# FFN's last projection: five of the eleven row pairs as seven block products instead of eight

## The chip, the cores and the metric

The kernel runs on one core of one Trainium2 chip. The metric is the device time of one execution in microseconds (us), as the median of several runs. A core has a matrix engine (TensorE, PE in the profile, with its weight loads as PEld), three engines for element-wise work (VectorE or DVE, ScalarE or ACT, GpSimd or POOL) and a queue that issues transfers (SyncE or SP). Each engine works through its own instructions in order and waits for the others by semaphores. SBUF is the working memory, PSUM the banks that PE writes its sums to.

## The reference

The reference is one block of a streaming encoder on 512 tokens with 1024 features: attention and a gated recurrence in parallel, merged, and then a feed-forward network with a final norm. Only its end matters here:

```
D_FF = ((8 * D_MODEL // 3 + 255) // 256) * 256          # 2816
...
        hn = rmsnorm(h, norm_ffn_g[l])
        gu = hn @ w_ffn_in[l]
        g, up = jnp.split(gu, 2, axis=-1)
        h = h + (jax.nn.silu(g) * up) @ w_ffn_out[l]
    return rmsnorm(h, final_norm_g)
```

So the last projection multiplies 512 x 2816 activations with a 2816 x 1024 matrix, adds the result to `h`, and each row of `h` is normed.

## The kernel before

Every float32 operand is split into a high part and a low remainder (`split`, L78): ACT writes the high part, DVE (or POOL, in `split_act`) subtracts it from the source to get the low one. A product of two such operands is three matmuls into the same PSUM sums (`mm3`, L72): high by high, high by low, low by high.

The 2816 rows of the last weight matrix are 22 tiles of 128, or eleven pairs. `act2[i]` holds the activations of pair i, transposed: 128 rows, two tiles, 512 tokens. The output is four tiles of 128 tokens (t) by two halves of 512 columns (cc). For the first half of the columns the loop (L1073 to L1098) goes over chunks of four row tiles; for each it takes the split weights (`weights`, L1084), and `out_tile` (L1038) adds its share to the four PSUM banks `po_out0` to `3` (tag `mm`, four banks). Activations are the stationary operand, 512 weight columns the moving one. Then `h_out` (L1044) adds each bank to `h`, squares it for the norm and multiplies by the norm's gain. The second half does the same with the last token tile cut into two pieces of 256 columns; its last chunks run piece by piece, so that each token tile can be normed and written out while the next one is still in PE.

Weights come in the order of `plan` (L94). `prefetch` takes them ahead of use: SP loads a piece of 512 KB into one of three `raw` buffers (`load`, L137), ACT and DVE split it into a `whl` buffer (four in the pool `wp`, more in another pool for some pieces, `extra`). A load waits until DVE has read the buffer's previous content, a split until PE has used the previous content of its `whl` buffer. `barrier` limits how far ahead this goes.

Before this stage the gate and up projections run as block products (`block_product`, L258): two by two blocks, seven products for eight. The last of them (`fu20`) ends among the first matmuls of the output stage. A framework orders the instructions of every engine by priorities and its own estimate of time; only the attention's PE order is fixed by hand (`manual_schedule`, L858). `split_act` (L1003) splits the activations; for pairs 0, 1, 2 and 4 POOL makes the low part.

Of the kernel before, what the change touches and what calls it, by code (L numbers as in the profile page):

```python
# [8 lines left out]
F32 = mybir.dt.float32  # L9
F32R = mybir.dt.float32r  # L10
# [4 lines left out]
P = 128  # L15
D = 1024
S = 512
KT = D // P
NT = S // P
# [3 lines left out]
FT = DFF // P  # L23
# [7 lines left out]
V_CW, V_CB, V_BR, V_BI, V_LAM, V_BM, V_GF = 0, 32, 40, 48, 56, 64, 80  # L31
NV = 88
CW = 256


@with_exitstack
def block_kernel(ctx: ExitStack, tc: tile.TileContext, x, norm_mix_g, w_in, b_merge, rel_table,
# [34 lines left out]
    def mm3(o, sh, sl, mh, ml, start, stop, parts=False):  # L72

        pe.matmul(o, sh, mh, start=start, stop=False, skip_group_check=parts)  # L74
        pe.matmul(o, sh, ml, start=False, stop=False, skip_group_check=parts)  # L75
        pe.matmul(o, sl, mh, start=False, stop=stop, skip_group_check=parts)  # L76

    def split(hi, lo, src):  # L78

        act.activation(hi, src, AF.Copy)  # L80
        dve.tensor_sub(lo, src, f(hi))  # L81
# [4 lines left out]

    def cols(src, col, width=CW):
        return (src, col, width)

    chunks = []  # L90
# [37 lines left out]
    for cc in range(2):  # L128
        for k0 in range(0, FT, 4):
            plan(f"fo{cc}_{k0}", cols(w_ffn_out, cc * S, S), rows=k0 * P, kts=min(4, FT - k0))  # L130

    made = []
    whole, every = slice(0, CW), slice(0, S)
# [27 lines left out]
    def weight_sums(name, ahead=False):  # L161
# [55 lines left out]
                blocks_[key] = o[:, i]  # L217
        return blocks_

    def prefetch(n):  # L220
        while len(made) < min(n, len(chunks), index.get(barrier[0], len(chunks))):
            name, parts, rows, kts = chunks[len(made)]
            if name in strassen:
                made.append(weight_sums(name))
                continue
            tiles = []
            wide = sum(width for *_, width in parts)
            step = 4 * CW // wide
            for k in range(0, kts, step):
                n_ = min(step, kts - k)  # L230
                if name in extra:
                    hl = extra[name].tile([P, 2, n_, wide], F32R, tag="whl", bufs=4, name=f"whl_{name}_{k}")
                else:
# [31 lines left out]

    def block_product(name, i, right, c):

        w = weights(name)
        p = ps.tile([P, 256], F32, tag="mm", bufs=4, name=f"p_{name}")
        q = ps.tile([P, 2, 256], F32, tag="st"[i % 2], bufs=2, name=f"q_{name}")  # L270
        a, b = (tg_.tile([P, 2, 256], F32, tag="tg", name=f"keep{n}_{name}") for n in "ab")

        def keep(o, src):
            act.activation(o, src, AF.Copy)
# [12 lines left out]
        dve.tensor_add(c[:, 0:2], q[:], a[:])  # L287
        product(p[:], w["a22"], right["t4"], False)
        keep(c[:, 2], p[:])
# [712 lines left out]

    def split_act(i):  # L1003
        o = act2[i]
        pl, bufs = (acp, 13) if i == 0 else (ohp, 6) if i < 7 else (op, 4)
        hi = pl.tile([P, 2, S], F32R, tag="act", bufs=bufs, name=f"act_hi{i}")
        lo = acp.tile([P, 2, S], F32R, tag="act", bufs=13, name=f"act_lo{i}")
        act.activation(hi[:], o[:], AF.Copy)  # L1008
        (pool if i in (0, 1, 2, 4) else dve).tensor_sub(lo[:], o[:], f(hi[:]))  # L1009
        for c in range(2):  # L1010
            actT[2 * i + c] = (hi[:, c], lo[:, c])
# [13 lines left out]
    hn_stack.close()  # L1025


    ohp = ctx.enter_context(pool_of("act_hi", 6, "right"))
    op = ctx.enter_context(pool_of("out", 4, "right"))
    for i, name in enumerate(n for n, *_rest in chunks if n.startswith("fo")):  # L1030
        if i % 4 >= 2:
            extra[name] = op
# [5 lines left out]
    def out_tile(t, po, k0, wf, at):  # L1038
        for k in range(min(4, FT - k0)):
            kk = k0 + k  # L1040
            mm3(po[:, 0:at.stop - at.start], actT[kk][0][:, t * P:(t + 1) * P], actT[kk][1][:, t * P:(t + 1) * P],
                wf(0, k, at), wf(1, k, at), kk == 0, kk == FT - 1)

    def h_out(cc, t, po, eng, i, at):  # L1044

        n = slice(cc * S + at.start, cc * S + at.stop)
        hs = ht[t][:, n]
        dve.tensor_add(hs, po[:, 0:at.stop - at.start], hs)
        junk = op.tile([P, S], F32, tag="junk", bufs=2, name=f"oj{t}_{i}")
        act.activation(junk[:, 0:at.stop - at.start], hs, AF.Square, accum_out=osq[t][:, i:i + 1])  # L1050
        eng.tensor_mul(hs, hs, g_fin[:, n])

    def out_norm(t, parts):

        part = cp.tile([P, 1], F32, tag="part", bufs=2, name=f"part{t}")
        if parts > 1:
            dve.tensor_reduce(part[:], osq[t][:, 0:parts], mybir.AxisListType.X, ALU.add)
            dve.tensor_scalar(part[:], part[:], 1.0 / D, EPS, ALU.mult, ALU.add)
        else:
            dve.tensor_scalar(part[:], osq[t][:, 0:1], 1.0 / D, EPS, ALU.mult, ALU.add)  # L1060
        return part

    def h_norm(t, part, i):
        sd = cp.tile([P, 1], F32, tag="sd", bufs=4, name=f"osd{t}")
        act.activation(sd[:], osq[t][:, i:i + 1], AF.Sqrt, bias=part[:], scale=1.0 / D)
        rs = cp.tile([P, 1], F32, tag="rs", bufs=4, name=f"ors{t}")
        dve.reciprocal(rs[:], sd[:])
        act.activation(ht[t][:, 0:384], ht[t][:, 0:384], AF.Copy, scale=rs[:, 0:1])
        dve.tensor_scalar(ht[t][:, 384:], ht[t][:, 384:], rs[:, 0:1], None, ALU.mult)
# [3 lines left out]
    ks = list(range(0, FT, 4))  # L1073
    late = 4
    for cc, tags in enumerate(("mmmm", "sstmm")):

        pieces = [(t, every) for t in range(NT)] if cc == 0 else [*((t, every) for t in range(3)), (3, slice(0, CW)), (3, slice(CW, S))]
        pos = [ps.tile([P, S], F32, tag={"m": "mm"}.get(tag, tag), bufs=4 if tag == "m" else 2, name=f"po_out{cc}_{i}")
               for i, tag in enumerate(tags)]
        for k0 in ks[:late] if cc else ks:  # L1080
            if cc == 0:
                for i in range(max(1, k0 // 2), min(k0 + 4, FT) // 2):
                    split_act(i)
            wf = weights(f"fo{cc}_{k0}", 3)  # L1084
            for (t, at), po in zip(pieces, pos):
                out_tile(t, po, k0, wf, at)
        if cc == 0:
            for (t, at), po in zip(pieces, pos):
                h_out(0, t, po, pool, 0, at)
    wfs = [weights(f"fo1_{k0}", 0) for k0 in ks[late:]]  # L1090
    for i, ((t, at), po) in enumerate(zip(pieces, pos)):
        for k0, wf in zip(ks[late:], wfs):
            out_tile(t, po, k0, wf, at)
        n = 1 + i // 4
        if i != 3:
            part = out_norm(t, n)
        h_out(1, t, po, dve, n, at)
        if i != 3:  # L1098
            h_norm(t, part, n)


# [23 lines left out]
```

## Time and profile before

| what | us |
|---|---|
| median of three runs (880.00 to 880.09) | 880.01 |
| the profiled execution's own time | 879.88 |
| its span, first to last instruction | 878.0 |
| PE busy | 868.9 |
| DVE busy | 545.3 |
| ACT busy | 471.4 |
| POOL busy | 115.1 |
| first output matmul starts | 746.75 |
| last output matmul starts | 871.6 |

The span is what the profile shows of one execution; the time also holds what lies around it, 1.88 us in this one. Times in the rows are counted from the span's start. A row of the timeline has the start, the duration, the engine, the line, the operation, and what is written from what; a number behind x says how many instructions were merged into it, and brackets tell how long the engine stood idle before and what ended that. Matmuls overlap: each is shown for longer than the distance to the next one, so the rate is read from starts. A row of the windows has, for each engine, busy time and (x) instructions, and at its end the clock granted to PE, the DMA engines' share and GB/s.

### The profile page before, as it was taken

Reading aid. Unit: us, or ns where it says so; the run is one execution under the profiler, and the core shown is the slowest. Engines: PE = TensorE matmul, PEld = TensorE weight load, DVE = VectorE, ACT = ScalarE, POOL = GpSimd, SP = SyncE. Lnnn points to the kernel's source line nnn. Section 1 sums busy time; section 2 is a strip of 40 time slices with the busy share of each in tenths; the row PEclk is TensorE's granted clock in tenths of the full one; section 3 lists DMA queues with packets and bytes.
Section 4 is the critical chain, followed back from the end, with each engine's and each line's share of the span. In section 5 each row is a group of like instructions: output and inputs, shape, how many; then the busy total and the mean of one; then the engine's idle time right before and its main releaser. Section 6 shows DMA issues by size and latency. Waiting matters only on the chain.

```text
span 878.0 us, 13349 instructions
## 1 busy us (share of the span) xinstructions
PE 868.9 (99%) x5220; PEld 775.8 (88%) x5220; DVE 545.3 (62%) x843; ACT 471.4 (54%) x827; POOL 115.1 (13%) x172
## 2 busy tenths in 40 slices
PE   9999999999999999999999999999999999999997
PEld 7988888888889889898888889999999999888886
DVE  5676456553456675766566557888888786554203
ACT  7586556642256675767633357555555555723103
POOL 3512212120113132322100000000000001401100
PEclk9999999999999999999999999999999999999999
DMA  8133322323332232332224622333333432363002
GB/s 285 56 121 98 94 81 88 121 96 96 108 97 84 85 96 73 97 97 61 74 95 131 229 94 74 110 109 97 97 96 112 127 100 72 113 198 120 26 1 97
DMA packets 86143, 90.10 MB, mean 103 GB/s; under 512 B 5456, under 2 KB 74672, under 8 KB 86080
## 3 DMA queue, kind: packets, MB, share of 16 engines
q1 hardware_dynamic: 84480, 85.73, 31.1%
q10 hardware_dynamic: 1376, 3.47, 1.1%
q8 instruction: 41, 0.67, 0.3%
q14 instruction: 22, 0.18, 0.1%
q0 software_dynamic: 224, 0.05, 0.0%
HBM read 87.10 MB, written 2.14 MB: 102 GB/s over the span
## 4 chain that ended last, share of the span: by engine, by line
PE 95%; DVE 2%; POOL 1%; ACT 1%; issue 0%; DMA 0%; ACTq 0%; DVEq 0%; POOLq 0%
PE po_out L74 4%; PE po_out L76 4%; PE po_out L75 4%; PE p_fg L76 2%; PE p_fg L75 2%; PE p_fg L74 2%; PE p_fu L75 2%; PE p_fu L76 2%; PE p_fu L74 2%; PE pT L806 2%; PE o L826 2%; PE po_v L74 2%; PE po_v L76 2%; PE po_v L75 2%; PE po_xr L75 2%; PE po_xr L74 2%
## 5 line engine op out<-in xcount | busy, mean ns | idle before, releaser
L75 PE MATMUL po_out<-whl_fo,act_hi 128*128 128x512 f32 (+1 forms) x198 | 72.4, 366 | 0.0
L74 PE MATMUL po_out<-whl_fo,act_hi 128*128 128x512 f32 (+1 forms) x198 | 72.4, 366 | 0.0
L76 PE MATMUL po_out<-whl_fo,act_lo 128*128 128x512 f32 (+1 forms) x198 | 71.7, 365 | 0.0
L81 DVE TENSOR_TENSOR whl_fo<-raw_fo,whl_fo 128x1024 fp32r<-128x1024 f32 x22 | 28.8, 1317 | 45.7 <-ACT whl_fo L80 45.2
L795 POOL TENSOR_SCALAR p<-p,rl 128x128 f32<-128x128 f32 (+1 forms) x64 | 36.9, 596 | 134.8 <-DVE rl L793 134.5
L1009 POOL TENSOR_TENSOR act_lo<-act,act_hi 128x1024 fp32r<-128x1024 f32 x4 | 11.4, 2842 | 324.0 <-ACT act_hi L1008 322.6
L80 ACT ACTIVATE whl_fo<-raw_fo 128x1024 fp32r<-128x1024 f32 x22 | 23.1, 1058 | 47.0 <-PE po_out L76 33.5
L75 PEld LDWEIGHTS po_out<-whl_fo,act_hi 128*128 128x128 f32 x198 | 37.4, 189 | 6.0
L76 PEld LDWEIGHTS po_out<-whl_fo,act_lo 128*128 128x128 f32 x198 | 37.3, 189 | 6.0
L74 PEld LDWEIGHTS po_out<-whl_fo,act_hi 128*128 128x128 f32 x198 | 37.4, 189 | 5.9
L792 ACT ACTIVATE p<-p,m 128x128 f32<-128x128 f32 (+1 forms) x64 | 35.8, 561 | 12.1 <-DVE m L791 11.8
L74 PE MATMUL po_v<-whl_v,xnT 128*128 128x256 f32 x128 | 36.5, 285 | 0.0
L76 PE MATMUL po_v<-whl_v,xnT 128*128 128x256 f32 x128 | 36.2, 283 | 0.0
L75 PE MATMUL po_v<-whl_v,xnT 128*128 128x256 f32 x128 | 36.2, 283 | 0.0
L791 DVE CUSTOM_DVE_ANT_0 p<-s,bias 128x128 f32<-128x128 f32 (+1 forms) x64 | 29.1, 484 | 1.0 <-PE s L783 1.0
L81 DVE TENSOR_TENSOR whl_qk<-raw_qk,whl_qk 128x1024 fp32r<-128x1024 f32 x16 | 20.9, 1307 | 13.4 <-ACT whl_qk L80 13.4
L81 DVE TENSOR_TENSOR whl_fu_s<-s_fu,whl_fu_s 128x1024 fp32r<-128x1024 f32 x20 | 24.1, 1222 | 6.2 <-ACT whl_fu_s L80 6.2
L81 DVE TENSOR_TENSOR pp<-pT,pp 128x384 fp32r<-128x384 f32 (+1 forms) x48 | 27.6, 597 | 0.5 <-ACT pp L80 0.4
L75 PE MATMUL po_xr<-xnT,whl_xr 128*128 128x512 f32 (+1 forms) x80 | 27.7, 353 | 0.0
L75 PE MATMUL po_gr<-xnT,whl_gr 128*128 128x512 f32 (+1 forms) x80 | 27.5, 347 | 0.0
L76 PE MATMUL po_gr<-xnT,whl_gr 128*128 128x512 f32 (+1 forms) x80 | 27.3, 347 | 0.0
L76 PE MATMUL po_xr<-xnT,whl_xr 128*128 128x512 f32 (+1 forms) x80 | 27.2, 346 | 0.0
(428 smaller groups left out, 3055.0 us busy)
## 6 DMA issues: line engine op xcount, KB each, us to landing
raw_fg<-in_w_ffn_in_dram SPq DMA_DIRECT2D x24, 512.0 KB, 4.2
raw_fu<-in_w_ffn_in_dram SPq DMA_DIRECT2D x22, 512.0 KB, 3.9
raw_fo<-in_w_ffn_out_dram SPq DMA_DIRECT2D x22, 512.0 KB, 4.4
raw_qk<-in_w_in_dram SPq DMA_DIRECT2D x32, 256.0 KB, 3.1
raw_xr<-in_w_in_dram SPq DMA_DIRECT2D x8, 512.0 KB, 3.7
raw_gr<-in_w_in_dram SPq DMA_DIRECT2D x8, 512.0 KB, 3.5
raw_ga<-in_w_in_dram SPq DMA_DIRECT2D x8, 512.0 KB, 3.6
raw_gb<-in_w_in_dram SPq DMA_DIRECT2D x8, 512.0 KB, 3.5
```

The source lines that it names most:

```text
L74: pe.matmul(o, sh, mh, start=start, stop=False, skip_group_check=parts)
L75: pe.matmul(o, sh, ml, start=False, stop=False, skip_group_check=parts)
L76: pe.matmul(o, sl, mh, start=False, stop=stop, skip_group_check=parts)
L80: act.activation(hi, src, AF.Copy)
L81: dve.tensor_sub(lo, src, f(hi))
L791: dve.tensor_tensor_reduce(prob[qb][:], scs[qb][:, 0:w], bias[:, S - w:S], -1.0, 3e38, ALU.add, ALU.min, nmax[:, qb:qb + 1])
L792: act.activation(prob[qb][:], prob[qb][:], AF.Exp, bias=nmax[:, qb:qb + 1], scale=-1.0, accum_out=lsum[:, qb:qb + 1])
L795: pool.tensor_scalar(prob[qb][:], prob[qb][:], rl[:, qb:qb + 1], 1.0, ALU.mult, ALU.mult)
L806: pe.transpose(pt[:, at * P:(at + 1) * P], prob[qb][:, kb * P:(kb + 1) * P], ident[:])
L826: pe.matmul(po[:, S - n:S], st, pp[i][:, part, lo:lo + n], start=kb == 0 and part == 0, stop=kb == NT - 1 and part == 1)
L1009: (pool if i in (0, 1, 2, 4) else dve).tensor_sub(lo[:], o[:], f(hi[:]))
```

## The change

Pairs 0 to 5 stay as they were (`plain`). Pairs 6 to 10 (`paired`) become block products in the form of Strassen and Winograd: the two 256-token halves and the two row tiles of a pair make a two by two matrix of activation blocks, the two row tiles and the two column halves one of weight blocks; seven products of blocks (256 tokens by 128 rows by 512 columns) give the four blocks of the output. Each product is six matmuls of 512 columns, where the pair had 48 in all.

- Weights: for a `paired` pair the pieces are `fo0` (both tiles of the first column half, as before), `t12` (T1 = w12 - w11 and T2 = w22 - T1), `t3b` (w22 - w12, and w22) and `t4` (w21 - T2), all made by `out_sums` with DVE subtractions, from three loads of 512 KB (one of them that of `fo0`) and two of 256 KB (`half`). Seven `whl` buffers are shared in a ring of seven (`out_home`): four in `wp`, three in the pool `out`.
- Activations: `a_first` splits the first token half of a pair into `left`; `a_sums` makes the sums of the activation blocks on DVE and splits them into `right`; `a_second` overwrites `left` and `a_last` part of `right` with the remaining differences. `spread` deals these out between the pairs' matmuls.
- Order: PE's order in the stage is fixed by hand: `fo0` of the plain pairs, `fo0` of the paired ones, three plain `fo1`, `t12`, three plain `fo1`, `t3b`, `t4`. Sums that several outputs share stay in PSUM (`p_out`, `q_out`) and are added to `h` at several points by `h_add`. The second column half is normed first; the last piece is the first column half of token tile 3, cut into two pieces of 256 columns.
- Chunks are one pair each now, `barrier` stops at `fo0_3`, and the last block product (`fu20`) reads two pieces ahead instead of one.

```
+N_PLAIN = 6
+OUT_TILES = (N_PLAIN - 1) + 2 * (11 - N_PLAIN)
...
+    for i in range(FT // 2):
+        plan_out(0, i)
+    for i in plain[:N_PLAIN // 2]:
+        plan_out(1, i)
+    for i in paired:
+        plan_block("t12", i)
+    for i in plain[N_PLAIN // 2:]:
+        plan_out(1, i)
+    for i in paired:
+        plan_block("t3b", i)
+    for i in paired:
+        plan_block("t4", i)
...
+    def out_home(name):
+        n = out_count[0] = out_count[0] + 1
+        pl, bufs = (wp, 4) if n % 7 in (1, 2, 3, 4) else (out_room[0], 3)
+        return pl.tile([P, 2, 2, S], F32R, tag="whl", bufs=bufs, name=f"whl_{name}")
...
+        if kind == "t12":
+            raw = wp.tile([P, 2, S], F32, tag="raw", bufs=3, name=f"raw_{name}")
+            sp.dma_start(out=raw[:], in_=w_ffn_out[rows:rows + P, :].rearrange("p (c n) -> p c n", c=2))
+            b22 = half_row(S)
+            t2 = t2_of[i] = out_room[0].tile([P, S], F32, name=f"t2_{i}")
+            t1 = raw[:, 1]
+            dve.tensor_sub(t1, raw[:, 1], raw[:, 0])
+            dve.tensor_sub(t2[:], b22, t1)
+            split(hl[:, 0, 0], hl[:, 1, 0], t2[:])
+            split(hl[:, 0, 1], hl[:, 1, 1], t1)
+        elif kind == "t3b":
+            raw = wp.tile([P, 2, S], F32, tag="raw", bufs=3, name=f"raw_{name}")
+            sp.dma_start(out=raw[:], in_=w_ffn_out[rows:rows + 2 * P, S:].rearrange("(k p) n -> p k n", p=P))
+            dve.tensor_sub(raw[:, 0], raw[:, 1], raw[:, 0])
+            split(hl[:, 0], hl[:, 1], raw[:])
+        else:
+            b21 = half_row(0)
+            t2 = t2_of.pop(i)
+            dve.tensor_sub(t2[:], b21, t2[:])
+            split(hl[:, 0, 0], hl[:, 1, 0], t2[:])
...
-        w = weights(name)
+        w = weights(name, 2 if name == strassen[-1] else 1)
...
-    barrier[0] = "fo0_16"
+    barrier[0] = "fo0_3"
...
+    def a_first(i):
+        o, left[i] = act2[i], pair_tile(i, "left")
+        split(left[i][:, :, 0], left[i][:, :, 1], o[:, :, 0:256])
+
+    def a_sums(i):
...
+        dve.tensor_add(s[:, 1], a21, a22)
+        dve.tensor_sub(s[:, 0], s[:, 1], a11)
+        dve.tensor_sub(a11, a11, a21)
+        dve.tensor_sub(a12, a12, s[:, 0])
+        split(right_[i][:, :, 0], right_[i][:, :, 1], s[:])
...
+    with tc.manual_schedule(engines={mybir.EngineType.PE}):
+
+        todo = [lambda i=i: a_first(i) for i in paired]
+        po = [bank("mm", f"po_out0_{t}") for t in range(NT)]
+        for i in plain:
+            if i:
+                split_act(i)
+            w = weights(f"fo0_{i}", 3)
+            for t in range(NT):
+                out_pair(po[t], t, i, w)
+            spread(todo, 1)
+        spread(todo, len(todo))
+        for t in (2, 3):
+            h_add(0, t, po[t][:])
+        pq = [bank("s", f"p_out{a}") for a in range(2)]
+        for n, i in enumerate(paired):
+            w = weights(f"fo0_{i}", 4)
+            for a in range(2):
+                out_block(pq[a][:], left[i], 0, a, w, 0, n == 0)
+            for a in range(2):
+                out_block(po[a][:], left[i], 1, a, w, 1, False)
+            a_sums(i)
+        for a in range(2):
+            h_add(0, a, pq[a][:])
+            h_out(0, a, po[a], pool, 0, every)
+        todo = [lambda i=i: a_second(i) for i in paired]
+        po = [bank("mm", f"po_out1_{t}") for t in range(NT)]
+        for i in plain[:half]:
+            w = weights(f"fo1_{i}", 4)
+            for t in range(NT):
+                out_pair(po[t], t, i, w)
+            spread(todo, 2)
+        spread(todo, len(todo))
...
+        ws = [weights(f"t4_{i}", 5) for i in paired]
+        for w, i in zip(ws, paired):
+            out_block(pq[0][:], right_[i], 0, 0, w, 0, False)
+        part = out_norm(2, 1)
+        h_out(0, 2, pq[0], dve, 1, every)
+        h_norm(2, part, 1)
+        for w, i in zip(ws, paired):
+            out_block(pq[1][:, 0:CW], right_[i], 0, 1, w, 0, False, slice(0, CW))
+        h_out(0, 3, pq[1], dve, 1, slice(0, CW))
+        part = out_norm(3, 2)
+        last = bank("mm", "po_last")
+        for n, (w, i) in enumerate(zip(ws, paired)):
+            out_block(last[:, 0:CW], right_[i], 0, 1, w, 0, n == 0, slice(CW, S))
+        h_out(0, 3, last, dve, 2, slice(CW, S))
+        h_norm(3, part, 2)
```

More of the change, by code (lines that the diff above doesn't have):

```diff
@@ L127, in block_kernel, with plan_out, plan_block @@
         plan(f"fu{j}", cols(w_ffn_in, DFF + j * P))
-    for cc in range(2):
-        for k0 in range(0, FT, 4):
-            plan(f"fo{cc}_{k0}", cols(w_ffn_out, cc * S, S), rows=k0 * P, kts=min(4, FT - k0))
+    plain, paired = list(range(N_PLAIN)), list(range(N_PLAIN, FT // 2))
+    def plan_out(cc, i):
+        plan(f"fo{cc}_{i}", cols(w_ffn_out, cc * S, S), rows=2 * i * P, kts=2)
+    def plan_block(kind, i):
+        plan(f"{kind}_{i}", rows=2 * i * P)
+    for i in range(FT // 2):
[10 more added lines that the diff above has]
+        plan_block("t4", i)
     made = []
@@ L218, in weight_sums, with out_sums, half_row @@
         return blocks_
+    out_count = [0]
+    out_room = [None]
+    t2_of = {}
+    def out_home(name):
+        n = out_count[0] = out_count[0] + 1
+        pl, bufs = (wp, 4) if n % 7 in (1, 2, 3, 4) else (out_room[0], 3)
+        return pl.tile([P, 2, 2, S], F32R, tag="whl", bufs=bufs, name=f"whl_{name}")
+    def out_sums(name, rows):
+        kind, i = name.split("_")
+        hl = out_home(name)
+        def half_row(col):
+            o = out_room[0].tile([P, S], F32, tag="half", bufs=3, name=f"half_{name}")
+            sp.dma_start(out=o[:], in_=w_ffn_out[rows + P:rows + 2 * P, col:col + S])
+            return o[:]
+        if kind == "t12":
[18 more added lines that the diff above has]
+            split(hl[:, 0, 0], hl[:, 1, 0], t2[:])
+        return lambda part, k, at=every: hl[:, part, k, at]
     def prefetch(n):
@@ L224, in prefetch @@
                 made.append(weight_sums(name))
+                continue
+            if not parts:
+                made.append(out_sums(name, rows))
                 continue
@@ L232, in prefetch @@
                     hl = extra[name].tile([P, 2, n_, wide], F32R, tag="whl", bufs=4, name=f"whl_{name}_{k}")
+                elif name[:2] == "fo":
+                    hl = out_home(name)
                 else:
@@ L1025, in block_kernel @@
     hn_stack.close()
[L1028 to L1032, printed above, removed]
+    ohp = ctx.enter_context(pool_of("act_hi", 1, "right"))
+    op = ctx.enter_context(pool_of("out", 1, "right"))
+    out_room[0] = op
     barrier[0] = None
@@ L1048, in h_out @@
         dve.tensor_add(hs, po[:, 0:at.stop - at.start], hs)
-        junk = op.tile([P, S], F32, tag="junk", bufs=2, name=f"oj{t}_{i}")
+        junk = tg_.tile([P, S], F32, tag="tg", name=f"oj{t}_{i}")
         act.activation(junk[:, 0:at.stop - at.start], hs, AF.Square, accum_out=osq[t][:, i:i + 1])
@@ L1071, in h_norm @@
         act.dma_start(out=out[t * P:(t + 1) * P, 0:384], in_=ht[t][:, 0:384])
[L1073 to L1099, printed above, removed]
+    def bank(tag, name):
+        return ps.tile([P, S], F32, tag=tag, bufs=4 if tag == "mm" else 2, name=name)
+    def spread(todo, n):
+        for _ in range(min(n, len(todo))):
+            todo.pop(0)()
```

61 lines of the change are left out of this document (55 added, 6 removed).

## The prediction

> **What bounds the kernel now.** I read the page first: busy shares, the 40 slices, the shares of the chain that ended last.
>
> ```profile
> span 878.0 us, 13349 instructions
> ...
> PE 868.9 (99%) x5220; PEld 775.8 (88%) x5220; DVE 545.3 (62%) x843; ACT 471.4 (54%) x827; POOL 115.1 (13%) x172
> ...
> DVE  5676456553456675766566557888888786554203
> ...
> PE 95%; DVE 2%; POOL 1%; ACT 1%; issue 0%; DMA 0%; ACTq 0%; DVEq 0%; POOLq 0%
> ```
>
> PE is 95% of the chain; DVE has room in the last six slices, the stage that changes. How tight PE is there I took from the tile view of `po_out` and from PE's timeline (start, duration):
>
> ```profile
> L76 PE MATMUL po_out<-whl_fo,act_lo x198: 279/389/396, 747.2 to 871.6; 128*128 128x512 f32 x154, 128*128 128x256 f32 x44
> ...
> 746.75 0.40 PE L74 MATMUL po_out<-whl_fo,act_hi 128*128 128x512 f32 x1
> ...
> 749.95 0.28 PE L74 MATMUL p_fu<-bt,whl_fu_s 128*128 128x256 f32 x1
> ...
> 751.27 0.28 PE L76 MATMUL p_fu<-bt,whl_fu_s 128*128 128x256 f32 x1
> ...
> 757.70 0.39 PE L74 MATMUL po_out<-whl_fo,act_hi 128*128 128x512 f32 x1
> ...
> 761.78 0.39 PE L75 MATMUL po_out<-whl_fo,act_hi 128*128 128x512 f32 x1
> ```
>
> From 757.70 to 761.78 lie 18 starts: 0.2267 us for 512 columns. From 749.95 to 751.27 lie 11: 0.12 us for 256. The stage has 3 x 154 = 462 and 3 x 44 = 132 of these, with 36 of the block products among them: 746.75 + 462 x 0.2267 + 168 x 0.12 = 871.65, where the last one starts. PE never waits; matmuls taken out are time gained, unless PE is made to wait.
>
> **What the change removes.** Five pairs go from 48 matmuls of 512 columns to 42; in the last piece 15 of these stand as 30 halves. That leaves 483 of 512 columns and 30 of 256: 109.5 + 3.6 = 113.1 us against 104.7 + 15.8 = 120.6: **7.5 us less PE**. The built order of the changed kernel has 81 fewer matmuls (594 - 513), so this is done; all five engines' orders are the same up to there.
>
> **What it adds: the entry.** The built order has two block products' ends among the first output matmuls, as before. What moves is ACT's queue.
>
> ```profile
> 728.77 2.40 POOL L1009 TENSOR_TENSOR act_lo<-act,act_hi 128x1024 fp32r<-128x1024 f32 x1 [300.69 <-ACT act_hi L1008]
> ...
> 737.75 0.62 ACT L80 ACTIVATE whl_fu_a<-raw_fu 128x512 fp32r<-128x512 f32 x1
> ...
> 751.87 1.05 ACT L1008 ACTIVATE act_hi<-act 128x1024 fp32r<-128x1024 f32 x1
> ...
> 755.06 0.28 PE L76 MATMUL p_fu<-bt,whl_fu_a 128*128 128x256 f32 x1
> ...
> 758.74 0.36 ACT L274 ACTIVATE c_u<-p_fu 128x256 f32<-128x256 f32 x1
> ```
>
> Before, `act_hi1` ran at 751.87. Now a weight split, `c_u` (which waits for PE's 755.06 + 0.28) and `left6` stand ahead of it, and behind it all of ACT's splits: 755.4 + 0.3 + 0.5 + 1.05 = 757.3. POOL then makes `act_lo1` in 2.40 us, ending at about 759.9 with a short wait for DVE. PE goes on at 755.2 with eight matmuls that need neither (1.8 us) and is at the first one on `act_lo1` at 757.0: **wait 3.0 us**. Both ends: 0 if ACT got ahead of `c_u`, which its order excludes; 3.5 if POOL loses another DVE operation.
>
> **What it adds: DVE's backlog.** DVE rows, a POOL row, the loads:
>
> ```profile
> 726.36 0.68 DVE L179 TENSOR_TENSOR s_fu<-s_fu,raw_fu 128x512 f32<-128x512 f32 x1
> 726.96 0.69 DVE L81 TENSOR_TENSOR whl_fg_a<-raw_fg,whl_fg_a 128x512 fp32r<-128x512 f32 x1
> ...
> 728.94 0.69 DVE L287 TENSOR_TENSOR c_u<-q_fu,keepa_fu 128x512 f32<-128x512 f32 x1 [0.69 <-ACT keepa_fu L274]
> 729.54 2.78 DVE L81 TENSOR_TENSOR whl_fu_a<-raw_fu,whl_fu_a 128x512 fp32r<-128x512 f32 x2
> ...
> 768.08 1.22 DVE L81 TENSOR_TENSOR whl_fo<-raw_fo,whl_fo 128x1024 fp32r<-128x1024 f32 x1
> 769.21 2.55 DVE L1009 TENSOR_TENSOR act_lo<-act,act_hi 128x1024 fp32r<-128x1024 f32 x2
> ...
> 871.33 0.43 DVE L1051 TENSOR_TENSOR h<-h,g_fin 128x256 f32<-128x256 f32 x1 [0.65 <-ACT oj L1050]
> 871.67 0.15 DVE L1057 TENSOR_REDUCE part<-osq 128x1 f32<-128x2 f32 x1
> ```
>
> ```profile
> 809.49 2.55 POOL L1051 TENSOR_TENSOR h<-h,g_fin 128x512 f32<-128x512 f32 x2 [45.99 <-ACT oj L1050]
> ```
>
> ```profile
> raw_fo<-in_w_ffn_out_dram SPq DMA_DIRECT2D x22, 512.0 KB, 4.4
> ```
>
> Start to start DVE takes 0.60 us for 512 elements, 1.13 for 1024, 0.34 for 256. And POOL holds DVE up: POOL's 2.40 us from 728.77 end at 731.17; the DVE operation on PSUM at 728.94 took its 0.69, but the SBUF pair issued at 729.54 took 2.78, which is 1.63 of waiting until 731.17 and then its own 1.2.
>
> [...]
>
> By the built order DVE has from 754.3 to the end of `fo1_0`'s split 12 operations of 1024, 10 of 512 and 17 of 256, `a_first` and `a_sums` among them: 13.6 + 6.0 + 5.8 = 25.4 us, and three POOL `act_lo` in between, 3 x 2.4 = 7.2: to 786.9, with small gaps 787.5. There a chain through the three `raw` buffers begins: `t12_6`'s load waits on SP for that split; + 4.4 = 791.9; two subtractions and an addition 1.8, `fo1_1`'s split 1.2 = 794.9; only then is `t12_7`'s load issued, with `t12_8`'s behind it on SP: 799.3. DVE waits for it at the head of its queue; behind it stand 17 operations of 512 (10.2 us), the last the addition that empties `po_out0_0`: **809.5**.
>
> PE: 759.9 + 22 x 0.2267 + 4 pairs x 24 + 5 block steps x 12 = 759.9 + 5.0 + 21.8 + 13.6 = 800.3, then two tiles of `fo1_0`, whose banks are those of `po_out0_2` and `_3`, long empty: 803.0. The third tile takes the bank of `po_out0_0`, as the built waits say: **wait 6.5 us**. Behind PE's wait stands everything. One tile later (1.4 us) the fourth waits for `po_out0_1`: five more DVE operations (3.0) and POOL's multiplication (2.55 / 2 = 1.3) in front: 4.3 - 1.4 = **2.9 us**.
>
> From there PE has 2 x 24 + 5 x 12 matmuls, 24.5 us, before it needs the next weight that isn't done (`fo1_3`); ahead of that DVE has some 6.5 us of work and at most two loads, 8.8. So I cost the other sums and splits, `a_second`, `a_last` and the 5 MB more of loads (10 x 512 and 10 x 256 KB more, 5 x 512 fewer) at nothing: PE's remaining 50 us of `fo1`, `t12` and `t3b` hide them, and if that cover were gone each late weight would cost its own split, some 1.2 us. Loads in 3.5 instead of 4.4 us would take 1.8 off the wait of 6.5, loads in 5.5 would add 2.2.
>
> **The clock.** Windows at the end, and the tile view of the first matmuls:
>
> ```profile
> 871.00:872.00 1.00, 0.92 (x8) 0.71 (x6) 0.63 (x4) 0.30 (x2) 0.00 (x0) 1.00 0.45 177
> ...
> 875.00:876.00 1.00, 0.00 (x0) 0.00 (x0) 0.00 (x0) 0.00 (x0) 0.00 (x0) 0.94 1.00 397
> 876.00:877.00 1.00, 0.00 (x0) 0.00 (x0) 0.00 (x0) 0.00 (x0) 0.00 (x0) 0.50 0.32 115
> ```
>
> ```profile
> L300 PE MATMUL busy<-idle x16: 379/630/634, 1.2 to 6.5; 128*128 128x512 bf16 x16
> ```
>
> PE stopped at 871.9 and the granted clock was halved at 875.9, 4.0 us later. At the start over half of 16 matmuls were slow (630 against 379 ns), some 3 to 4 us. A wait of 6.5 us passes 4.0, so PE restarts slow and loses 1.5 to 2.0; six slow matmuls fall into the second wait and hide about 1.2. I take **0.8**, between 0 and 3.
>
> [...]
>
> **The tail.**
>
> ```profile
> 861.02 1.28 ACT L1065 ACT_TABLE_LOAD   x1
> ...
> 862.91 0.55 DVE L1069 TENSOR_SCALAR h<-h,ors 128x640 f32<-128x640 f32 x1
> ...
> 871.96 0.42 DVE L1048 TENSOR_TENSOR h<-po_out,h 128x256 f32<-128x256 f32 x1
> ...
> 873.55 0.61 ACT L1068 ACTIVATE h<-h,ors 128x384 f32<-128x384 f32 x1 [0.30 <-DVE ors L1067]
> ```
>
> Before, the last addition starts as PE ends. Now four `h` tiles end within PE's last 15 x 0.2267 + 30 x 0.12 = 7.0 us: ten DVE operations of 512, three of 256, three of 640, small ones: 6.0 + 1.0 + 1.4 + 0.5 = 8.9, begun 1.8 earlier, level with PE; the waits for squares and the 1.28 us table add up to 1.4. **1.2 us later**, between 0 and 1.4.
>
> **Sum:** -7.5 + 3.0 + 6.5 + 2.9 + 0.8 + 1.2 = +6.9. The profiled execution took 879.88 us, 1.88 around its span, and the median is 880.01, so one sum serves both: **886.8 us**.
>
> **Rivals.** (1) *DVE is in time* (faster): `po_out0_0` is emptied by 803.0. Then 1.6 of the last wait at most, no clock loss: -7.5 + 3.0 + 1.6 + 1.2 = -1.7, 878.2; with the entry covered too 875. It decides once waits and tail sum to less than 5.7. It needs no POOL hold-up and both loads in 3 us; the load row is against it. 5%. (2) *POOL doesn't hold DVE up that much*: `fo1_0`'s split then ends with its buffer: PE leaves `fo0_4` at 781.3, + 1.05 + 1.2 = 783.6, + 4.4 + 3.0 + 4.4 + 10.2 = 805.6: wait 2.6, then 1.6; -7.5 + 2.8 + 2.6 + 1.6 + 1.2 = +0.7, 880.6. For it: before, most POOL spans met an idle DVE. 13%. (3) *The clock stays low, or loads share the queue*: 2 to 5 us more, 889 to 892. 14%. That the matmuls aren't fewer is excluded by the built order.
>
> **How the numbers follow.** Forecast 68%, 883.5 to 889; rival 1 5%, 2 13%, 3 14%. Range 880.4 to 891. A difference under 0.2% can't be told from none here: faster 0.05; same 0.11, most of rival 2; slower 0.84.
>
> **What would show it.** PE idle near 757 behind POOL `act_lo`, and near 803 to 810 and once more behind DVE `h`; DVE gap at the `t12_7` load; DVE's SBUF operations stretched under POOL's; granted clock 0.5 after the long gap; PE's po_out work 113 us. No gap at the third tile, or gaps at `t12` or `t3b`, would make it wrong.

## The result and the profile after

| | before | after |
|---|---|---|
| median, us | 880.01 | 883.89 (883.72 to 884.65, five runs) |
| the profiled execution's own time, us | 879.88 | 883.89 |
| its span, us | 878.0 | 882.1 |
| PE busy, us, and instructions | 868.9, 5220 | 863.6, 5139 |
| DVE busy, us | 545.3 | 594.3 |

The changed kernel takes 1.0046 of the time before, with a 95% interval from 1.0031 to 1.006: slower by 4 us. The forecast was 886.8 in a range from 880.4 to 891.0. The side and the place were right; the size was 2.9 us too much.

The page of the changed kernel, at the lines that were shown of before:

```profile
span 882.1 us, 13360 instructions
...
PE 863.6 (98%) x5139; PEld 768.0 (87%) x5139; DVE 594.3 (67%) x928; ACT 485.9 (55%) x857; POOL 112.8 (13%) x170
...
DVE  5666556663456675766557458888887885888655
PEclk9999999999999999999999999999999999998999
...
PE 88%; DVE 6%; ACT 2%; DMA 1%; issue 1%; POOL 1%; DVEq 0%; ACTq 0%; POOLq 0%
```

81 matmuls are gone, as the built order said, and PE is busy for 5.3 us less. But the chain that ended last was 95% PE and is now 88%: DVE has 6% of it, and three slices before the end the granted clock is an 8. So PE no longer sets the end alone. What stopped it can be read from PE's waits from 740 to the end (what waits, for what, us in total, times, longest); the kernel before has none there:

```profile
PE po_out L76 <- DVE h L1147: 5.9, 1, 5.9
PE po_out L78 <- POOL act_lo L1075: 1.8, 1, 1.8
PE po_out L76 <- ACT c_u L340: 0.5, 1, 0.5
```

Three waits: at the entry for `c_u` and for POOL's `act_lo1`, and in the middle for DVE's addition `h`, which empties the bank of `po_out0_0`. None at `t12`, `t3b` or `t4`. The large one, in PE's timeline:

```profile
802.90 0.39 PE L78 MATMUL po_out<-whl_fo,act_lo 128*128 128x512 f32 x1
809.15 0.79 PE L76 MATMUL po_out<-whl_fo,act_hi 128*128 128x512 f32 x1 [5.86 <-DVE h L1147]
...
811.45 0.63 PE L78 MATMUL po_out<-whl_fo,act_lo 128*128 128x512 f32 x1
812.16 0.79 PE L76 MATMUL po_out<-whl_fo,act_hi 128*128 128x512 f32 x1
...
813.04 0.39 PE L78 MATMUL po_out<-whl_fo,act_lo 128*128 128x512 f32 x1
```

At full speed the next matmul would have started at 803.13; it starts 6.0 later. Six matmuls (the third tile) then take 0.43 each from start to start instead of 0.2267, and the fourth tile follows at 812.16. What DVE did meanwhile:

```profile
787.02 0.68 DVE L1141 TENSOR_TENSOR h<-po_out,h 128x512 f32<-128x512 f32 x1
791.70 0.69 DVE L265 TENSOR_TENSOR raw_t<-raw_t 128x512 f32<-128x512 f32 x1 [3.99 <-DMA raw_t<-in_w_ffn_out_dram]
...
798.78 0.69 DVE L265 TENSOR_TENSOR raw_t<-raw_t 128x512 f32<-128x512 f32 x1 [2.32 <-DMA raw_t<-in_w_ffn_out_dram]
...
808.41 0.68 DVE L1147 TENSOR_TENSOR h<-po_out,h 128x512 f32<-128x512 f32 x1
...
811.42 0.68 DVE L1147 TENSOR_TENSOR h<-po_out,h 128x512 f32<-128x512 f32 x1
```

This is the chain of the forecast, each link within a microsecond: backlog until 787.0, then the two loads of `t12_6` and `t12_7`, for which DVE stands 3.99 and 2.32 us, then sixteen operations 0.60 apart, and the addition for `po_out0_0` at 808.41, that for `po_out0_1` at 811.42. The granted clock, in windows of half a microsecond (after PE's busy time the clock, the DMA share and GB/s):

```profile
805.50:806.00 0.50, 0.00 (x0) 1.00 0.80 270
806.00:806.50 0.50, 0.00 (x0) 0.55 0.87 352
...
812.50:813.00 0.50, 0.50 (x2) 0.63 0.94 320
813.00:813.50 0.50, 0.50 (x4) 1.00 0.94 320
```

The windows between these show 0.50. So a mean of 0.55 means half speed from 806.05, and 0.63 half speed until 812.87: 6.8 us.

### The profile page after: what moved, and what is told of

Read it like the earlier page. It is cut to its first block, busy times and chain, and to the rows that moved or that the text cites. A ratio compares the mean times of both kernels' runs of the same rounds, so it can differ in the third digit from the quotient of the medians.

```text
span 882.1 us, 13360 instructions
## 1 busy us (share of the span) xinstructions
PE 863.6 (98%) x5139; PEld 768.0 (87%) x5139; DVE 594.3 (67%) x928; ACT 485.9 (55%) x857; POOL 112.8 (13%) x170
## 4 chain that ended last, share of the span: by engine, by line
PE 88%; DVE 6%; ACT 2%; DMA 1%; issue 1%; POOL 1%; DVEq 0%; ACTq 0%; POOLq 0%
PE p_fu L78 2%; PE p_fg L78 2%; PE p_fg L77 2%; PE p_fg L76 2%; PE p_fu L77 2%; PE p_fu L76 2%; PE pT L872 2%; PE o L892 2%; PE po_v L76 2%; PE po_v L78 2%; PE po_v L77 2%; PE po_xr L76 2%; PE po_xr L77 2%; PE po_gr L76 2%; PE po_k L76 2%; PE po_gr L78 2%
## 5 line engine op out<-in xcount | busy, mean ns | idle before, releaser
L76 PE MATMUL po_out<-whl_fo,act_hi 128*128 128x512 f32 x96 | 38.7, 403 | 6.4 <-DVE h L1147 5.9
L78 PE MATMUL po_out<-whl_fo,act_lo 128*128 128x512 f32 x96 | 38.0, 395 | 1.8 <-POOL act_lo L1075 1.8
L77 PE MATMUL po_out<-whl_fo,act_hi 128*128 128x512 f32 x96 | 37.9, 395 | 0.0
L76 PEld LDWEIGHTS po_out<-whl_fo,act_hi 128*128 128x128 f32 x96 | 18.4, 191 | 11.7 <-DVE h L1147 7.1
L77 PE MATMUL po_xr<-xnT,whl_xr 128*128 128x512 f32 (+1 forms) x80 | 27.7, 353 | 0.0
L77 PE MATMUL po_gr<-xnT,whl_gr 128*128 128x512 f32 (+1 forms) x80 | 27.5, 347 | 0.0
L78 PE MATMUL po_gr<-xnT,whl_gr 128*128 128x512 f32 (+1 forms) x80 | 27.3, 347 | 0.0
L78 PE MATMUL po_xr<-xnT,whl_xr 128*128 128x512 f32 (+1 forms) x80 | 27.2, 346 | 0.0
L76 PE MATMUL po_gr<-xnT,whl_gr 128*128 128x512 f32 (+1 forms) x80 | 27.1, 347 | 0.0
L83 DVE TENSOR_TENSOR whl_fg_s<-s_fg,whl_fg_s 128x1024 fp32r<-128x1024 f32 x20 | 24.0, 1222 | 4.2 <-ACT whl_fg_s L82 4.0
L76 PE MATMUL po_xr<-xnT,whl_xr 128*128 128x512 f32 (+1 forms) x80 | 26.3, 351 | 0.4 <-ACT xnT L534 0.4
L83 DVE TENSOR_TENSOR whl_fo<-raw_fo,whl_fo 128x1024 fp32r<-128x1024 f32 x17 | 20.6, 1220 | 9.0 <-ACT whl_fo L82 9.0
```

## The experiments

**Free banks.** The theory: the loss is PE's wait for two banks that DVE empties late. The rival: DVE is late for everything, and PE would stand at the next thing.

```
-        po = [bank("mm", f"po_out1_{t}") for t in range(NT)]
+        po = [bank("mm" if t < 2 else "t", f"po_out1_{t}") for t in range(NT)]
...
-        qq = [bank("t", f"q_out{a}") for a in range(2)]
+        qq = [bank("mm", f"q_out{a}") for a in range(2)]
```

> The third and fourth tile of the first plain pair of the second half (po_out1_2, po_out1_3) get two free banks, and q_out gets the banks of po_out0_0 and po_out0_1, which it needs 14 us later. Theory (the loss of the changed kernel is PE's wait for these two banks, with the halved clock behind it): PE's waits of 5.9 and 0.3 us near 803 to 812 go, the clock stays at 1.00 and about 2.1 us of slow matmuls go too: 883.9 - 5.9 - 2.1 = 875.9 us, under the kernel before. Rival (VectorE is simply behind by 6 us at this point, and whatever PE needs next of it is late as well, the weights of t12 first): PE stands at the next place instead, near 816, and the time stays above 880.

Measured: 875.78 us (ratio to before 0.9957, interval 0.9944 to 0.9969). PE's waits of this kernel in the same stretch:

```profile
PE po_out L78 <- POOL act_lo L1075: 1.8, 1, 1.8
PE po_out L76 <- ACT c_u L340: 0.5, 1, 0.5
```

The wait for `h` is gone and nothing has come in its place; the two of the entry are left. 8.1 us for other banks, with no work changed: this settles the main cause. The same block products are faster than the kernel before by 4 us when the additions may be late.

**POOL's part in DVE's backlog.**

```
-        (pool if i in (0, 1, 2, 4) else dve).tensor_sub(lo[:], o[:], f(hi[:]))
+        (pool if i == 0 else dve).tensor_sub(lo[:], o[:], f(hi[:]))
```

> act_lo of pairs 1, 2 and 4 is made by VectorE instead of POOL. Theory (POOL holds VectorE up): three VectorE rows of the changed kernel lost 2.1, 2.2 and 2.2 us (2.48 and 2.63 for 0.42, 3.50 for 1.29), 6.5 in all; three more operations of 1024 cost 3.4; the backlog is 3.1 us shorter, the wait for the bank of po_out0_0 falls from 5.9 to about 2.8, which is too short for the clock to be halved: about 879 to 880.5 us. Rival (the load chain through the raw buffers sets the wait, POOL does not matter): wait of 5 to 6 us as before, 883 to 884. Rival (VectorE pays for the three operations and nothing comes back): wait about 9 us, 887.

Measured: 879.74 us (0.9999 to 1.0018), the median of eleven executions in two groups: six took 879.1 to 879.7 us, five 881.6 to 882.6. The profile is of one of the six. First the DVE rows of the changed kernel, then those of this one, from its timeline:

```profile
757.67 2.48 DVE L1119 TENSOR_TENSOR act<-act 128x256 f32<-128x256 f32 x1
760.07 2.63 DVE L1120 TENSOR_TENSOR act<-act,s 128x256 f32<-128x256 f32 x1
```

```profile
757.67 0.42 DVE L1119 TENSOR_TENSOR act<-act 128x256 f32<-128x256 f32 x1
758.02 0.42 DVE L1120 TENSOR_TENSOR act<-act,s 128x256 f32<-128x256 f32 x1
758.35 1.22 DVE L1075 TENSOR_TENSOR act_lo<-act,act_hi 128x1024 fp32r<-128x1024 f32 x1
...
804.39 0.69 DVE L1147 TENSOR_TENSOR h<-po_out,h 128x512 f32<-128x512 f32 x1
```

The same two operations take 0.42 us when POOL is still, and 2.48 and 2.63 beside POOL's `act_lo` operations (757.50 to 762.43). DVE takes on three operations more and is 4.0 us earlier at the addition (804.39 for 808.41). PE's two waits at the banks are then 2.2 and 1.3 us. The POOL hold-up was real: by the medians, taking it away gave 4.1 of the 8.1 us that the free banks gave; by the means, which count both groups, 3.4 of 8.0.

**The entry, three times.** In the changed kernel `left6` is the first tile of a pool of 15, and by the built waits it follows ScalarE's earlier work, with `act_hi1` behind it. A first edit gives the `act_hi` tiles a pool of their own, ahead of `left` and `right`:

```
     ohp = ctx.enter_context(pool_of("act_hi", 1, "right"))
+    prp = ctx.enter_context(pool_of("pairs", 1, "right"))
...
-        pl, bufs = (acp, 13) if i == 0 else (ohp, OUT_TILES)
+        pl, bufs = (acp, 13) if i == 0 else (ohp, N_PLAIN - 1)
...
-        return ohp.tile([P, 2, 2, 256], F32R, tag="act", bufs=OUT_TILES, name=f"{name}{i}")
+        return prp.tile([P, 2, 2, 256], F32R, tag="pair", bufs=OUT_TILES - N_PLAIN + 1, name=f"{name}{i}")
```

> act_hi of the plain pairs gets a pool of its own, opened first, and left and right one behind it; by the built order ScalarE then makes act_hi1 to act_hi5 ahead of c_u, as in the kernel before, and POOL begins act_lo1 about 3 us earlier. Theory (VectorE's queue sets when po_out0_0 is emptied, however early PE comes): the entry wait falls from 2.9 us to 0.5 or less, and the wait at the bank grows by about the same, to some 8 us: 882.5 to 884. Rival (the two waits add up, as my sum had them): 883.9 - 2.5 = 881.4 or less.

> Both edits of the first and the third run: two pools, and free banks for po_out1_2 and po_out1_3. Theory: without the bank wait the entry's 2.5 us are worth their full size, so 875.9 - 2.5 = 873.4 us, and PE's idle time between 747 and 870 is under 1 us. Rival (the weights of the block products are next, VectorE being as far behind): the entry's gain is lost again to a wait for weights, 875.5 to 876.

Measured: 882.47 us (1.0018 to 1.0039) with the old banks, 879.07 (0.998 to 0.9997) with the free ones. The second missed by 5.7 us. The first lies at the edge of its range, but not for the reason given there, and so by luck: the wait at the entry did not fall, it grew, and the waits at the banks did not grow to 8 us but came to 2.5 in all. ScalarE's timeline (of the first of the two) shows why:

```profile
754.06 1.99 ACT L1074 ACTIVATE act_hi<-act 128x1024 fp32r<-128x1024 f32 x2
...
755.95 2.93 ACT L1074 ACTIVATE act_hi<-act 128x1024 fp32r<-128x1024 f32 x3
758.79 0.36 ACT L340 ACTIVATE c_u<-p_fu 128x256 f32<-128x256 f32 x1
```

Five `act_hi` run ahead of `c_u`, which empties PE's bank for the fourth tile: PE waits 3.8 us for `c_u`, where the changed kernel loses 2.9 to `c_u` and `act_lo1` together. In the kernel before, ScalarE had this same order, with `c_u` at 758.74, and PE did not wait: by the code it had four row tiles for each token tile, twice the matmuls, before it came to that bank. And the clock was halved; half-microsecond windows of the kernel with both edits:

```profile
757.00:757.50 0.50, 0.00 (x0) 0.93 0.94 238
757.50:758.00 0.50, 0.00 (x0) 0.50 0.94 197
...
764.00:764.50 0.50, 0.50 (x3) 0.74 0.00 0
```

Half speed from 757.43 to 764.26. PE restarts at 759.33 and works 4.9 us at half speed, 2.45 lost, with no second wait to hide in. With the 3.3 by which the wait for `c_u` is longer that makes 5.75, and this kernel's profiled execution (879.26) lies 5.6 above the run below that has the same banks and only the 0.5 for `c_u` (873.7): the whole miss. Five of its eleven executions took 877.9 to 878.8, at a granted clock of 0.996 to 0.997 over the span for the 0.994 of the others, so the share of the clock differs from one to the next.

With the old banks the same loss at the entry does no harm (882.47 is under 883.89). PE comes to the third tile 3.5 us later than in the changed kernel and still goes on 1.2 earlier, at 807.99 for 809.15, because VectorE's addition starts at 807.25 for 808.41:

```profile
807.99 0.50 PE L76 MATMUL po_out<-whl_fo,act_hi 128*128 128x512 f32 x1 [1.18 <-DVE h L1148]
```

So only `act_hi1` should go ahead:

```
+    hi1p = ctx.enter_context(pool_of("act_hi1", 1, "right"))
     ohp = ctx.enter_context(pool_of("act_hi", 1, "right"))
...
-        pl, bufs = (acp, 13) if i == 0 else (ohp, OUT_TILES)
+        pl, bufs = (acp, 13) if i == 0 else (hi1p, 1) if i == 1 else (ohp, OUT_TILES - 1)
...
-        return ohp.tile([P, 2, 2, 256], F32R, tag="act", bufs=OUT_TILES, name=f"{name}{i}")
+        return ohp.tile([P, 2, 2, 256], F32R, tag="act", bufs=OUT_TILES - 1, name=f"{name}{i}")
```

> Only act_hi1 gets a pool of its own, opened first; by the built order it alone now runs on ScalarE ahead of c_u and left6 (at about 754.0 instead of 756.3), and c_u stays where it was. Banks as in the changed kernel. Theory (waits of PE don't add up ahead of a time that VectorE's queue sets): the entry wait falls by about 1.8 us, PE comes to the bank of po_out0_0 at about 801, still waits for an addition at 808 to 809, and the time stays at 883 to 884.5. Rival (the two waits are separate prices, as my sum had them): 883.9 - 1.8 = 882.1 or less.

Measured: 883.68 us (1.003 to 1.0058). PE's waits:

```profile
PE po_out L76 <- DVE h L1148: 6.8, 1, 6.8
PE po_out L76 <- ACT c_u L340: 0.5, 1, 0.5
```

The wait for `act_lo1` is gone, the one for the bank has grown from 5.9 to 6.8, and the time is the same within the interval. The profiled execution is the shortest of five (882.44 to 884.84): in it PE comes to the third tile 2.0 us earlier and goes on 1.1 earlier, and that 1.1 is VectorE's, whose addition starts at 807.34 for 808.41. So in the changed kernel the entry wait itself costs nothing that these executions can show: PE only waits later. With the free banks the edit is worth its size:

> The same pool for act_hi1, and free banks for po_out1_2 and po_out1_3. Theory: without a time set by VectorE behind it the entry wait is worth its size: 875.8 - 1.8 = 874.0, PE's 0.5 us for c_u left. Rival (what ScalarE or VectorE has then given up makes another step late): 875.5 or more.

Measured: 873.7 us (0.9916 to 0.9941), 2.1 under the run with the banks alone. PE waits only the 0.5 us for `c_u`. The version with `act_lo` on DVE as well (the POOL edit above):

> As the run before, and act_lo of pairs 1, 2 and 4 on VectorE. By the built order act_lo1 stands ahead of the last act product there and is done by about 756.5, ahead of PE's need at 757.0. Theory: 873.5 to 874.0, no PE wait but the 0.5 us for c_u. Rival (act10 and the splits behind act_lo1 are 1.1 us late and PE meets that): 874.5 to 875.5.

Measured: 873.53 us (0.9914 to 0.9939): as the theory had it, and not to be told from the run before it. Once PE doesn't wait for the bank, POOL's hold-up is free.

**The order on VectorE.**

```
-    with tc.manual_schedule(engines={mybir.EngineType.PE}):
+    with tc.manual_schedule(engines={mybir.EngineType.PE, mybir.EngineType.DVE}):
```

> VectorE's operations of this stage are kept in the order in which the program gives them, like PE's; banks and pools as in the changed kernel. The additions that empty po_out0_0 and po_out0_1 then stand ahead of the sums and splits of t12_7 to t12_10 and of a_second, not behind them. The work on VectorE is the same. Theory (what stands ahead in VectorE's queue sets the wait, not how much work it has): the additions run at about 801.5 to 803, PE's waits there go, the clock stays: 875.5 to 876.5. Rival (VectorE's amount of work sets it): PE stands instead at the weights of t12, and the time stays above 880.

Measured: 898.34 us (1.0193 to 1.0221). A miss, and not a test of the theory: in the program's order the additions for `po_out0_2` and `_3` come early, and DVE stood for PE at the first of them:

```profile
787.28 0.69 DVE L1141 TENSOR_TENSOR h<-po_out,h 128x512 f32<-128x512 f32 x1 [12.64 <-PE po_out L78]
```

After that DVE was further behind than before: PE waited 7.9 us at the bank and 8.5 for the last `t4` weight. So those two additions were moved behind the sums of the last pair:

```
-        for t in (2, 3):
-            h_add(0, t, po[t][:])
         pq = [bank("s", f"p_out{a}") for a in range(2)]
...
             a_sums(i)
+        for t in (2, 3):
+            h_add(0, t, po[t][:])
```

> As the run with VectorE in program order, but the additions of po_out0_2 and po_out0_3, for which VectorE stood 12.6 us there, are issued behind the sums of the last pair. VectorE's work is unchanged, and no bank or pool is. Theory (the order of VectorE's queue sets the wait at the bank, the amount of work does not, as long as VectorE doesn't stand): the additions that empty po_out0_0 and po_out0_1 run within 2 us of PE's end with them, at 800.5 to 803, PE's waits of 5.9 and 0.3 us and the slow clock go: 875.5 to 877. Rival (amount of work): PE stands at the third tile or at the weights of t12 by 3 us or more, 880 or above.

Measured: 888.44 us (1.0086 to 1.0114), which by the number alone is the rival. PE's waits:

```profile
PE p_out L76 <- ACT whl_t L82: 8.5, 1, 8.5
PE po_out L78 <- POOL act_lo L1075: 1.8, 1, 1.8
PE po_out L76 <- DVE h L1141: 1.3, 1, 1.3
```

At the bank the theory held. The additions for `po_out0_0` and `_1` start at 803.24 and 804.63, PE's waits for them are gone with the same work on DVE, and PE does not wait at `t12`. The 1.3 us (L1141) are for the bank of `po_out0_2`, whose addition this edit moved back. What took the place of the bank wait is a wait of 8.5 us from 865 on for the last `t4` weight, which this order puts on DVE behind the closing additions of `h`, and, from PE's restart at 873.40 to 878.5, slow matmuls (256 columns every 0.21 us, then every 0.12). The order of DVE's queue can remove the bank wait; the program's order as it stands is not the one. That another order would keep both waits away is not shown: none was tried, since the free banks need none.

**What the clock costs in the changed kernel.** 24 matmuls that nobody reads keep PE busy during the wait:

```
+                if i == 0 and t == 2:
+                    spin = bank("t", "spin")
+                    for _ in range(24):
+                        pe.matmul(spin[:], actT[0][0][:, 0:P], w(0, 0, every), start=True, stop=True)
                 out_pair(po[t], t, i, w)
```

> 24 matmuls of 512 columns into a bank that is free then (5.4 us, nobody reads the result) are put into PE's queue where it waits for the bank of po_out0_0, so that the wait stays but the clock should not be halved. Theory (the slow matmuls fall into the wait for po_out0_1 and hide in it; the clock costs only what is slow after 812.2, about 0.4 us, and the second bank 1.7): 883.2 to 883.7. Rival (the clock is the price, the second bank nearly nothing, as the two idle times of 5.9 and 0.3 us say): 881.8 to 882.2.

Measured: 883.56 us (1.0027 to 1.0052), 0.3 less than the changed kernel. PE's timeline:

```profile
804.81 5.60 PE L1214 MATMUL spin<-whl_fo,act_hi 128*128 128x512 f32 x24
810.25 0.39 PE L76 MATMUL po_out<-whl_fo,act_hi 128*128 128x512 f32 x1
...
812.13 0.50 PE L76 MATMUL po_out<-whl_fo,act_hi 128*128 128x512 f32 x1 [0.36 <-DVE h L1147]
```

The 24 matmuls hold PE 1.1 us longer than the wait did, the third tile then runs at full speed, and the fourth starts at 812.13, where it started at 812.16 after six slow matmuls: DVE's second addition sets it (811.40 here, 811.42 there). The six slow matmuls cost nothing; what the clock cost is the few behind them. This execution also shows once more that PE's arrival does not matter: its clock was halved at the entry for 3.4 us, PE came to the third tile 1.7 us later than in the changed kernel, and the end did not move.

**Three pairs instead of five.** `N_PLAIN = 8` on top of the free banks and the pool for `act_hi1`.

> Three pairs as block products instead of five, with the pool for act_hi1 and the free banks (the run with these two edits and five pairs took 873.7 us). Theory (a pair is worth six matmuls of 512 columns, 1.36 us, as nothing else is on the path): 873.7 + 2 x 1.36 = 876.4, with 0.5 either way. Rival (VectorE's load costs something with each pair): 875.5 or less.

Measured: 880.5 us (1.0002 to 1.002), 4.1 more than the theory and 5.0 more than the rival's bound. Two things came along that neither had. PE's timeline has a new wait at the entry, behind POOL's `act_lo2`:

```profile
763.36 0.39 PE L77 MATMUL po_out<-whl_fo,act_hi 128*128 128x512 f32 x1
765.58 0.50 PE L78 MATMUL po_out<-whl_fo,act_lo 128*128 128x512 f32 x1 [1.83 <-POOL act_lo L1075]
...
869.97 0.28 PE L78 MATMUL po_last<-whl_t,right 128*128 128x256 f32 x1
```

That is 2.0 us. The last matmul starts at 869.97 against 865.05 with five pairs: 4.9 later, of which 2.0 is this wait and 2.7 are 12 matmuls of 0.2267, as forecast. The other 1.9 lie behind PE: from its last matmul to the end of the span 8.7 us against 6.8. A likely reason, which no run tests, is that the `t4` stage is now three pairs long and covers less of DVE's norming. A pair's matmuls are worth their 1.36 us on PE, but a number of pairs also moves the entry and the tail.

**The best version.** Free banks, the pool for `act_hi1`, `act_lo` on DVE, and `po_out0_3` in a bank of tag `t`, so that PE doesn't need `c_u`:

```
-        po = [bank("mm", f"po_out0_{t}") for t in range(NT)]
+        po = [bank("mm" if t < 3 else "t", f"po_out0_{t}") for t in range(NT)]
```

> The pool for act_hi1, the free banks, act_lo on VectorE, and po_out0_3 in a bank that is free when PE comes to it, so that it does not wait 0.5 us for c_u. Theory: 873.5 - 0.5 = 873.0 us. Rival (PE then meets act_lo1 or act_hi1 instead): 873.5.

Measured: 873.16 us, ratio 0.9923 (0.991 to 0.9937): 0.6% to 0.9% faster than before. It is 0.4 us under the same kernel without this edit, and none of PE's waits is left. The windows of this kernel and of the changed one over the same 60 us (busy us and instructions of PE, PEld, DVE, ACT, POOL, then the clock):

```profile
754.00:784.00 30.00, 30.00 (x138) 24.60 (x137) 29.23 (x44) 18.55 (x25) 0.00 (x0) 1.00 0.60 196
784.00:814.00 30.00, 30.00 (x134) 24.86 (x133) 27.59 (x43) 13.47 (x22) 2.83 (x2) 1.00 0.59 193
```

```profile
754.00:784.00 30.00, 27.75 (x126) 22.45 (x125) 29.86 (x39) 16.93 (x24) 8.11 (x3) 1.00 0.47 151
784.00:814.00 30.00, 24.06 (x99) 18.98 (x98) 23.43 (x34) 12.96 (x21) 3.78 (x2) 0.89 0.56 182
```

PE is never idle, although DVE is busy for 57 us of the 60. The last matmul starts at 864.46, 7.1 us ahead of the 871.6 before, and the tail behind it is 0.4 longer: the 6.8 us. Of the 7.5 that the change takes off PE nearly all has come through.

## Why the prediction was right, and where its sizes were off

- **7.5 us less PE: right.** With all waits gone the best version has 7.1 of it. In the changed kernel 128.5 us lie between the first and the last start of the stage (746.77 to 875.24); without the 4.3 of block products and the 11.0 lost at the entry and the banks, 113.1 are left, as forecast.
- **Entry, 3.0:** the row is right: PE was at the first matmul on `act_lo1` at 759.92, and without the two waits it would have been there at 757.0, so 2.9. But the sum took it as a price of its own, and the run with `act_hi1` alone shows that it is not: with most of it gone (0.5 for `c_u` is left) the median stays. In the changed kernel PE's arrival at the third tile doesn't matter within some 6 us. Entry 3.0 and bank 6.5 are really one term, the time at which DVE's addition lets PE go on. The sum is right all the same, since the wait of 6.5 was reckoned from the arrival that the entry had delayed.
- **First bank wait, 6.5:** 6.0 measured. PE's arrival (803.0 forecast, 803.1), the end of the backlog (787.5, 787.0), the landing of `t12_7` (799.3, 798.8) and the last addition (809.5, some 809.1) came out as worked out. The row of the POOL hold-up that it leant on was tested and held; the two load waits are read from the trace alone, and no run took one of them away.
- **Second bank wait 2.9 and clock 0.8: this is the step that failed in size.** From 809.15 on PE lost 2.1, not 3.7. The step put "five more DVE operations (3.0) and POOL's multiplication (2.55 / 2 = 1.3) in front". The five operations were there (808.41 to 811.42, 3.0). POOL's multiplication was not in front: DVE's operations stayed 0.60 apart, and it was POOL that was held up.

The POOL row of the changed kernel, and DVE's first operation that was stretched, from their timelines:

```profile
809.93 2.71 POOL L1150 TENSOR_TENSOR h<-h,g_fin 128x512 f32<-128x512 f32 x1 [38.42 <-ACT oj L1149]
```

```profile
812.02 1.17 DVE L83 TENSOR_TENSOR whl_t<-raw_t,whl_t 128x512 fp32r<-128x512 f32 x1
```

A POOL operation that took 1.27 in the kernel before, where DVE had no operation on two SBUF operands beside it, took 2.71 here and ended at 812.64. That is 1.22 after DVE began the addition at 811.42, which has one operand in PSUM. In four other runs this distance is 1.22 to 1.24 as well (free banks, two pools, `act_hi1` alone, PE kept busy), so POOL most likely stood until DVE came to that addition, and then took its 1.27. Without those 1.3 us the second wait is 3.0 - 1.4 = 1.6, and the slow matmuls hide inside it, leaving 0.3 to 0.5 for the clock: the 2.1 measured.

- **Tail, 1.2:** 0.5 measured. From PE's last matmul start to the end of the span 878.0 - 871.6 = 6.4 before, 882.1 - 875.2 = 6.9 after. So, by the sizes, most of the 1.4 of waits and table load was covered; which part, no run separates.

With the measured sizes the sum is -7.5 + 2.9 + 6.0 + 1.7 + 0.4 + 0.5 = +4.0, the profiled execution's 883.89 - 879.88. Every term that missed was too large, so the forecast was not right by errors that cancel.

- **Rivals.** That POOL doesn't hold DVE up (880.6) is excluded for this kernel, and the run that takes POOL out landed at 879.74, close to what that rival's sum gave, in part by chance: VectorE has three operations more there (3.4 us) that the rival did not count. That DVE is in time (875 to 878) came true once the additions were allowed to be late. A clock that stays low was seen in the first of the two DVE orders: halved at 807.75 and still at 0.50 in the window that ends at 816.0, 8.2 us at least. In the changed kernel half speed lasted 6.8 us, but most of that cost nothing, since PE stood or had a second wait ahead.

## What to carry to other kernels

Before a stage is made cheaper on the bound engine, look at who empties the banks that it will reuse: here 7.5 us of saved matmuls were lost to banks that a 67% busy engine emptied late, the first by 6 us, and giving two tiles other banks brought them back. Waits of one engine ahead of a time that another engine sets are not added up; price the latest one, and expect an edit at an earlier wait to do little until it is gone. When an engine's queue is reordered to free one wait, read who then waits longest behind it, since the same order cost 8.5 us at the other end of the stage.

## What the runs showed of the hardware

Where both its ends could be timed, the halved clock lasted 3.4 us or twice that, and it didn't need a long wait. Half speed lasted 6.8 us in the changed kernel (806.05 to 812.87), 6.8 in the run with two pools and free banks (757.43 to 764.26), 3.4 in the run with VectorE in program order (759.96 to 763.38), and 3.4 in the run with PE kept busy (761.52 to 764.93), whose one-microsecond windows are these:

```profile
758.00:759.00 1.00, 0.22 (x1) 0.00 (x0) 1.00 (x1) 1.00 (x3) 1.00 (x1) 1.00 0.61 238
759.00:760.00 1.00, 0.01 (x1) 0.01 (x1) 1.00 (x1) 1.00 (x2) 0.94 (x1) 1.00 0.97 377
760.00:761.00 1.00, 1.00 (x4) 0.85 (x5) 1.00 (x2) 1.00 (x2) 0.98 (x1) 1.00 1.04 393
761.00:762.00 1.00, 1.00 (x5) 0.79 (x4) 1.00 (x1) 1.00 (x2) 1.00 (x1) 0.76 1.07 412
...
764.00:765.00 1.00, 1.00 (x4) 0.80 (x3) 0.97 (x3) 1.00 (x2) 0.00 (x0) 0.53 0.09 12
```

PE had stood for about 1.8 us, was at work again from 760.0, and the clock fell at 761.5, for 3.4 us. In the changed kernel the same pause at the entry left the clock at 1.00. So 1.8 us came before a halving in one run and not in another, and what decides it no run shows. Nor is the 4.0 us of the forecast's row a fixed delay: in the changed kernel the clock fell 2.8 us after PE stopped (803.29 to 806.05). Two runs have two falls each that can be timed: 759.96 and 807.75 in the run with VectorE in program order, and in the changed kernel 806.05 and, after PE's last matmul, 877.72. The distances, 47.79 and 71.67 us, are 14.0 and 21.0 times the 3.41 of the run with PE kept busy. Two distances don't make a rule.

The run with `act_lo` on DVE, whose pauses in the profiled execution are 2.2 us at most, seems to have both cases: its six shorter executions have a granted clock of 0.998 to 0.999 over the span, its five longer ones 0.994 to 0.997. No trace of a longer one shows where. That a wait of 2.8 us is too short for the clock to be halved, as that run's expectation has it, was the author's estimate, and the 1.8 us above speak against it. What a halving costs depends on what follows: one cost 2.45 us where nothing followed it and 0.3 where a second wait did.
